# Modulation products behind their sums, and new places for VectorE and ScalarE work, in a three-layer float32 network

## The chip, the cores and the metric

The kernel runs on one core of a Trainium2 chip. The metric is the device time of one execution in microseconds (us); smaller is better. Inputs and outputs are float32 in the chip's main memory. TensorE multiplies in the fp32r type: each float32 matrix is held as a sum of two such values, "hi" and "lo", and a product is made of three matmuls (hi x hi, lo x hi, hi x lo).

## The reference, cut to what matters

512 tokens `x` and 256 context tokens, width 1024, pass two layers whose norms are modulated by a vector `c`, then a third block without modulation.

```python
for layer in range(2):
    mod_x = split(silu(c) @ ada_w[layer] + ada_b[layer], 6)       # ada_w: 1024 x 6144 a layer
    mod_c = split(silu(c_ctx) @ ada_w[layer] + ada_b[layer], 6)   # layer 1 needs mod_c[0], mod_c[1] only
    hx = rms_norm(x, norm1_g[layer]) * (1 + mod_x[1]) + mod_x[0]
    # layer 0: mLSTM heads with gate scans, beside a short gated convolution, over context and x
    # layer 1: 16 query heads in groups on 4 key heads, rms_norm and rope on q and k, softmax
    x = x + mod_x[2] * mixer(hx)
    x = x + mod_x[5] * mlp(rms_norm(x, norm2_g[layer]) * (1 + mod_x[4]) + mod_x[3])   # relu squared, hidden 4096
# third block
u = rms_norm(x, norm_mix_g) @ w_in
mixed = concat(rms_norm(stick_breaking(u)), rms_norm(conformer_conv(u)), rms_norm(s5_ssm(u)))
x = x + mixed @ w_out
x = x + cross_attention(x, mem);  x = x + gated_ffn(x)
```

Stick-breaking attention has 8 heads and takes, for each score, a softplus and then sums of the softpluses of all later keys.

## The kernel before, in words

TensorE (PE) does nearly everything that takes time, in an order written out by the program and, outside the grouped attention and the sums of stick-breaking, refined by a scheduler. The other engines feed it. Each engine takes its instructions in the order given.

**Weights.** `load_w` brings a unit of up to 2048 columns a partition by one DMA of SP's queue into `wst`; ScalarE (ACT) casts it to `whi` (L347), VectorE (DVE) subtracts to `wlo` (L348), in four pieces of 528, 528, 528 and 464 columns. `fm` (matmuls L310) and `tm` (L340) are the two loops of products. `split(hi, lo, src, ce, se)` is this pair of instructions for any tensor: `ce`, ACT by default, casts (L347), `se`, VectorE by default, subtracts (L348).

**Modulation.** `ada_v` makes `silu(c) @ ada_w` off TensorE: for each of six items of 1024 columns it brings rows of `ada_w` through two staging tiles (`ada`) and multiplies and adds them into accumulators `mac` (DVE, L500; the first row by ACT). In layer 0 an item has two variants (for x and for the context), two halves, four row pairs each. When both halves of an item are summed, sixteen or eight small matmuls (`ada_rows`, L472) gather the accumulators of all partitions, and `ada_end` writes `mods` (L458, L465). There are four `mac` buffers. `ada_v` is a generator, one step for each row pair, in the list `fillers`; `pump()` takes one step, and `fm` and `tm` pump behind each unit of weights (`steps`), or amid a product where `mix` is given.

**MLP of layer 0.** 8 blocks of 512 hidden columns: in each, four products with `w1` (m0 to m3 here), whose results go through ACT (relu and square) and a split into `h` on DVE (L347 cast, L348 subtraction), then eight products with `w2` that read `h`. Their results are added to x by DVE (L570). Layer 1's modulation runs in `fillers` beside them, two steps behind each unit.

**Around grouped attention.** `AT_ORD` is a string read from the left before the attention loop: a digit u is the query projection `q_proj(u)`, t a step of `key_turn` (transposes L1098 of keys, casts L1103), r a step of the rope of `q_rope(0)` (L1060, L1072, L1073), p a step of `at_prep(0)`. A capital letter hands the generator to `waiting`, and `fm`/`tm` then step it amid products (`wait_step`). `at_prep(c)` transposes queries (L1123), casts them (L1129, L1130), takes row maxima of scores (matmuls L1139, reductions L1140), turns these (L1149) and casts them (L1151) as a row of `QL` that the scores L1159 need. It yields after each of eight score tiles but the first, and `N_Y` = 3 times before L1149.

**Third block.** `sb_prep` makes queries and keys of stick-breaking heads (transposes L1643 and L1647, ACT L1650 and L1656, DVE L1651 and L1657); `sb_scores` makes scores (L1669 to L1671) and softplus (ACT L1677 and L212, DVE L1680, split); L1773 sums and ACT makes weights `w` (L212); L1787 multiplies values. `yhl` is the state-space branch's output, split, which the product `ssm_glu_w` reads; `OC` holds the convolution branch's output (`ev_pw`, L1725). `stage` brings the first 256 columns of a weight matrix early, in `ada` tiles, and its `part(i)` splits a quarter.

## Time and profile before

| | |
|---|---|
| median of 3 runs | 2483.6 us (2482.04 to 2489.34) |
| profiled execution | 2484.28 us, of which the span (first to last instruction) 2482.5 us and 1.78 us outside it |
| mean granted TensorE clock | 0.989 of full speed |
| busy: PE, DVE, ACT, POOL | 98%, 63%, 38%, 5% of the span |

A time at an instruction is from the start of the span. "Idle before" is how long its engine stood before it, and what released it. [...]

### The profile page before, as it was taken

Reading aid. Unit: us, or ns where it says so; the run is one execution under the profiler, and the core shown is the slowest. Engines: PE = TensorE matmul, PEld = TensorE weight load, DVE = VectorE, ACT = ScalarE, POOL = GpSimd, SP = SyncE. Lnnn points to the kernel's source line nnn. Section 1 sums busy time; section 2 is a strip of 40 time slices with the busy share of each in tenths; the row PEclk is TensorE's granted clock in tenths of the full one; section 3 lists DMA queues with packets and bytes.
Section 4 is the critical chain, followed back from the end, with each engine's and each line's share of the span. In section 5 each row is a group of like instructions: output and inputs, shape, how many; then the busy total and the mean of one; then the engine's idle time right before and its main releaser. Section 6 shows DMA issues by size and latency. Waiting matters only on the chain.

```text
span 2482.5 us, 34516 instructions
## 1 busy us (share of the span) xinstructions
PE 2424.4 (98%) x13648; PEld 2005.8 (81%) x13648; DVE 1572.1 (63%) x3300; ACT 940.8 (38%) x1982; POOL 118.9 (5%) x172
## 2 busy tenths in 40 slices
PE   7999999999999999999999999999999999999999
PEld 6978889888888889954487888886877977888887
DVE  5688467565543336799777775488767666543442
ACT  4322563322222214456543232342486534322321
POOL 0000110000000000133200000000000000000000
PEclk9999999999999999999999999999999999999999
DMA  7535034245442122100222323333103522323322
GB/s 249 171 111 161 1 102 136 69 127 171 145 136 68 52 68 86 56 1 1 66 93 87 116 85 102 102 102 99 57 1 128 178 69 85 102 74 105 101 86 93
DMA packets 214770, 238.46 MB, mean 96 GB/s; under 512 B 10704, under 2 KB 166992, under 8 KB 214608
## 3 DMA queue, kind: packets, MB, share of 16 engines
q1 hardware_dynamic: 212880, 233.19, 29.5%
q10 hardware_dynamic: 1728, 3.07, 0.3%
q8 instruction: 107, 1.75, 0.3%
q14 instruction: 55, 0.45, 0.1%
HBM read 225.63 MB, written 8.39 MB: 94 GB/s over the span
## 4 chain that ended last, share of the span: by engine, by line
PE 87%; DVE 7%; ACT 2%; DMA 2%; POOL 1%; issue 1%; SPq 0%; ACTq 0%; POOLq 0%; DVEq 0%
PE ps L310 65%; PE ps L340 6%; PE ps L897 2%; PE ps L646 2%; DMA ada<-ada_w 1%; PE ps L1249 1%; PE ps L865 1%; DVE mx L1140 1%; PE ps L1773 1%; PE ps L1557 1%; PE ps L1159 1%; DVE wlo L348 1%; PE ps L395 1%; PE ps L386 1%; PE ps L1468 1%
## 5 line engine op out<-in xcount | busy, mean ns | idle before, releaser
L310 PE MATMUL ps<-a,whi 128*128 128x512 f32 (+1 forms) x3784 | 986.7, 356 | 2.5 <-ACT a L405 1.4
L310 PEld LDWEIGHTS ps<-a,whi 128*128 128x128 f32 x3784 | 641.8, 189 | 111.4 <-issue 7.6
L310 PE MATMUL ps<-a,wlo 128*128 128x512 f32 (+1 forms) x1980 | 641.1, 357 | 0.0
L347 ACT CAST whi<-wst 128x528 fp32r<-128x528 f32 (+3 forms) x611 | 338.2, 610 | 579.0 <-PE ps L310 481.6
L310 PE MATMUL ps<-h,whi 128*128 128x512 f32 (+1 forms) x1776 | 458.0, 353 | 3.8 <-DVE h L347 3.7
L348 DVE TENSOR_TENSOR wlo<-wst,whi 128x528 fp32r<-128x528 f32 (+3 forms) x611 | 391.3, 677 | 77.5 <-ACT whi L347 76.5
L310 PEld LDWEIGHTS ps<-a,wlo 128*128 128x128 f32 x1980 | 346.5, 189 | 54.8 <-issue 1.9
L310 PEld LDWEIGHTS ps<-h,whi 128*128 128x128 f32 x1776 | 295.8, 189 | 54.7 <-DVE h L347 7.5
L310 PE MATMUL ps<-h,wlo 128*128 128x512 f32 (+1 forms) x800 | 239.1, 349 | 0.0
L570 DVE SCALAR_TENSOR_TENSOR a<-ps,mods,a 128x512 f32<-128x512 f32 (+1 forms) x200 | 122.2, 641 | 156.0 <-PE ps L310 155.4
L340 PE MATMUL ps<-whi,a 128*128 128x256 f32 (+1 forms) x1024 | 191.2, 285 | 0.6 <-ACT a L1590 0.6
L500 DVE SCALAR_TENSOR_TENSOR mac<-ada,sc,mac 128x512 f32<-128x512 f32 x224 | 158.5, 748 | 37.7 <-DMA ada<-ada_w 21.4
L340 PEld LDWEIGHTS ps<-whi,a 128*128 128x128 f32 x1024 | 160.8, 191 | 11.3 <-issue 7.9
L310 PEld LDWEIGHTS ps<-h,wlo 128*128 128x128 f32 x800 | 134.6, 189 | 19.7
L340 PE MATMUL ps<-wlo,a 128*128 128x256 f32 (+1 forms) x512 | 145.3, 285 | 0.5 <-DVE wlo L348 0.5
L559 ACT ACTIVATE t<-ps 128x512 f32<-128x512 f32 x60 | 35.9, 598 | 256.4 <-PE ps L310 243.9
L347 DVE CAST h<-t 128x512 fp32r<-128x512 f32 x60 | 25.5, 425 | 149.7 <-ACT t L561 149.7
L340 PEld LDWEIGHTS ps<-wlo,a 128*128 128x128 f32 x512 | 97.6, 191 | 2.1 <-issue 1.1
L352 POOL TENSOR_TENSOR sm<-sm,mhalf 128x2 f32<-128x2 f32 (+2 forms) x27 | 28.5, 1056 | 973.4 <-DVE sm L388 970.3
L212 ACT ACTIVATE p<-ps 128x512 f32<-128x512 f32 x96 | 53.8, 596 | 40.1 <-PE ps L1160 30.2
L1140 DVE TENSOR_REDUCE mx<-ps 128x1 f32<-128x512 f32 (+1 forms) x128 | 62.8, 550 | 4.9 <-PE ps L1139 4.6
L2021 DVE TENSOR_TENSOR a<-a,ps 128x512 f32<-128x512 f32 x16 | 11.0, 688 | 79.9 <-PE ps L310 79.9
(433 smaller groups left out, 2974.2 us busy)
## 6 DMA issues: line engine op xcount, KB each, us to landing
wst<-mlp_w SPq DMA_DIRECT2D x64, 1024.0 KB, 5.1
ada<-ada_w SPq DMA_DIRECT2D x80, 512.0 KB, 4.1
wst<-ffn_w_in SPq DMA_DIRECT2D x20, 1024.0 KB, 5.0
wst<-ffn_w_out SPq DMA_DIRECT2D x16, 704.0 KB, 4.2
wst<-hyb_w_in SPq DMA_DIRECT2D x10, 1024.0 KB, 5.6
wst<-w_in SPq DMA_DIRECT2D x9, 1024.0 KB, 5.2
a<-ada_w SPq DMA_DIRECT2D x32, 256.0 KB, 5.4
wst<-att_w_in SPq DMA_DIRECT2D x6, 1024.0 KB, 5.0
```

The source lines that it names most:

```text
L212: i = A.activation(out, in_, func, **kw)
L310: T.matmul(p, w(k, slice(m, m + P)), tiles[t][i // 2][:, s:s + n], start=(k == k0 and i == 0), stop=(k == k1 and i == 2))
L340: T.matmul(p, tiles[i // 2][:, s:s + P], (wl if i == 1 else wh)(k, slice(0, n)), start=(k == 0 and i == 0), stop=(k == KC - 1 and i == 2))
L347: last["copy"] = (ce.copy if ce is A else ce.tensor_copy)(hi, src)
L348: return se.tensor_tensor(lo, src, f(hi), ALU.subtract)
L352: G.tensor_tensor(r, v, mhalf[:, :n], ALU.pow)
L500: V.scalar_tensor_tensor(m, x, s, m, op0=ALU.mult, op1=ALU.add)
L559: A.activation(r, p, AF.Relu)
L570: V.scalar_tensor_tensor(xs, p, mod(l, 5)(c, v), xs, op0=ALU.mult, op1=ALU.add)
L646: T.matmul(vp[n_][:, u * 256:(u + 1) * 256], act[k][t][i // 2][:, s:s + P], (lo if i == 1 else hi)[:, k, :], start=(k == 0 and i == 0 and ...
L897: T.matmul(o, x, VS[:, kt, h, :], start=(n_ == 0), stop=(n_ == len(terms) - 1))
L1140: V.tensor_reduce(MX[:, e, t, i:i + 1], z, AX.X, ALU.max)
```

## The change

Four edits. (1) In `ada_v` the gathering matmuls of an item may come `ADA_LATE` = 2 steps behind its last sum, if the accumulators held meanwhile fit in the buffers; layer 0 gets six `mac` buffers, so all its items come two steps later; in layer 1 with four buffers items 2 to 5 do. (2) The MLP of layer 0 pumps amid each `w1` product (behind its fourth of eight row blocks) instead of behind each `w1` unit, and not at all in block 0's `w1` products. (3) `AT_ORD` is written anew: two key turns fewer and the maxima sooner; the rest of the key turns is handed to the products; in the first turn of `at_prep` only every second score tile yields, and `N_Y` there is 1. (4) In the third block the key casts of `sb_prep`, the copy out of `ev_pw` and the casts of the staged `w_out` go from ACT to DVE, and the splits of `yhl` stand before the projection of values.

```diff
+ADA_LATE = 2
-AT_ORD = "1ttttrrrr2pppP3"
+AT_ORD = "1ttrrrrT2pP3"
-    def stage(src):
+    def stage(src, ce=A):
-            split(*hl, sts[i // 2][:, (i % 2) * 512:(i % 2 + 1) * 512])
+            split(*hl, sts[i // 2][:, (i % 2) * 512:(i % 2 + 1) * 512], ce)
-                                if mix and k % mix == mix - 1:
+                                if mix and (k == at if at is not None else k % mix == mix - 1):
                                     pump()
-    def ada_v(fp, l, its, after=None):
+    def ada_v(fp, l, its, after=None, bufs=4):
+        late = []
+        def end(i, vs, accs):
+            p = ps()[:, :256]
+            for v in vs:
+                ada_rows(p, pick[:, v, :], lambda j: accs[j // 2][v][:, (j % 2) * 256:(j % 2 + 1) * 256], v == 0, v == vs[-1])
+            ada_end(l, i, p)
...
             if k0 == KC - 2 and h:
-                p = ps()[:, :256]
-                for v in vs:
-                    ada_rows(p, pick[:, v, :], lambda j: accs[j // 2][v][:, (j % 2) * 256:(j % 2 + 1) * 256], v == 0, v == vs[-1])
-                ada_end(l, i, p)
+                held = len(vs) * 2 + (len(range(2 if l == 0 or i + 1 < 2 else 1)) * (2 if l else 1))
+                late.append((n_ + (ADA_LATE if held <= bufs else 0), (i, vs, accs)))
+            if late and late[0][0] <= n_:
+                end(*late.pop()[1])
+            yield
+        if late:
+            end(*late.pop()[1])
             yield
-            fm(w1[:, b * blk * P:(b + 1) * blk * P], KC, act, rngs, evac1, c0=b * blk, first=groups if b == 0 else None, steps=steps)
+            fm(w1[:, b * blk * P:(b + 1) * blk * P], KC, act, rngs, evac1, c0=b * blk, first=groups if b == 0 else None,
+               steps=0 if amid else steps, mix=amid and b > 0, at=3 if amid else None)
-    fillers.append(ada_v(fp, 0, range(2, 6), began))
+    fillers.append(ada_v(fp, 0, range(2, 6), began, 6))
-                if (e, t) != (0, 0):
+                if (t % 2 if c == 0 else (e, t) != (0, 0)):
                     yield
-        for _ in range(N_Y):
+        for _ in range(N_Y if c else 1):
             yield
-                A.copy(ks[u], k[u])
+                V.tensor_copy(ks[u], k[u])
+    yhl = new_act(2, False)
+    for c in range(2):
+        split(*yhl[c][0], Y[c])
     psum.close()
     psum = open_psum(6)
...
-        A.copy(OC[c], items[0][1])
+        V.tensor_copy(OC[c], items[0][1])
-    staged = stage(a["w_out"][:, 0:256])
+    staged = stage(a["w_out"][:, 0:256], V)
```

In layer 0, DVE's queue behind the gate scans reads so before the change (L753 to L767 belong to the scans; `mac_1727` is the last sum of the item whose gathering matmuls come next on PE, `wlo_2008` a weight unit that PE reads soon):

```order
L753 SCALAR_TENSOR_TENSOR a_1780<-a_1774,a_1781 4x512
L756 SCALAR_TENSOR_TENSOR a_1780<-a_1774,a_1781 4x512
...
L766 TENSOR_SCALAR a_1819<-a_1781 64x256
L500 SCALAR_TENSOR_TENSOR mac_1727<-ada_1872,sc,mac_1727 128x512
L767 SCALAR_TENSOR_TENSOR a_1819<-a_1781,a_1819 64x256
L500 SCALAR_TENSOR_TENSOR mac_1952<-ada_1902,sc,mac_1952 128x512
L500 SCALAR_TENSOR_TENSOR mac_1953<-ada_1902,sc,mac_1953 128x512
L465 TENSOR_TENSOR mods_92<-ps_1919,cols 128x8 x2
L348 TENSOR_TENSOR wlo_2008<-wst_2006,whi_2007 128x528 x3
```

And so in the changed kernel, whose lines stand 2 to 15 further down here (L511 is L500, L350 is L348, L768 to L782 are the scans):

```order
L768 SCALAR_TENSOR_TENSOR a_1780<-a_1774,a_1781 4x512
L771 SCALAR_TENSOR_TENSOR a_1780<-a_1774,a_1781 4x512
...
L781 TENSOR_SCALAR a_1819<-a_1781 64x256
L511 SCALAR_TENSOR_TENSOR mac_1937<-ada_1938,sc,mac_1937 128x512
L782 SCALAR_TENSOR_TENSOR a_1819<-a_1781,a_1819 64x256
L511 SCALAR_TENSOR_TENSOR mac_1936<-ada_1938,sc,mac_1936 128x512
L511 SCALAR_TENSOR_TENSOR mac_1937<-ada_1938,sc,mac_1937 128x512
L350 TENSOR_TENSOR wlo_2008<-wst_2006,whi_2007 128x528 x3
```

The last sum of the item has gone from behind the scans to ahead of them; what stands behind them now are sums of the next item and then the weight unit.

In the MLP of layer 0, block 2, DVE's queue around the split of m3's result (`h_6170`, `h_6172`) reads so before:

```order
L500 SCALAR_TENSOR_TENSOR mac_6612<-ada_6613,sc,mac_6612 128x512 x2
L500 SCALAR_TENSOR_TENSOR mac_6612<-ada_6617,sc,mac_6612 128x512 x2
L500 SCALAR_TENSOR_TENSOR mac_6612<-ada_6763,sc,mac_6612 128x512
L347 CAST h_6170<-t_6175 128x512
L500 SCALAR_TENSOR_TENSOR mac_6612<-ada_6763,sc,mac_6612 128x512
L348 TENSOR_TENSOR h_6171<-t_6175,h_6170 128x512
L347 CAST h_6172<-u_6181 128x256
```

And so now (`h_6161`, `h_6163` are the same tensors):

```order
L511 SCALAR_TENSOR_TENSOR mac_6300<-ada_6301,sc,mac_6300 128x512
L511 SCALAR_TENSOR_TENSOR mac_6300<-ada_6305,sc,mac_6300 128x512 x2
L349 CAST h_6161<-t_6166 128x512
L511 SCALAR_TENSOR_TENSOR mac_6300<-ada_6433,sc,mac_6300 128x512
L350 TENSOR_TENSOR h_6162<-t_6166,h_6161 128x512
L349 CAST h_6163<-u_6172 128x256
```

One staged tile's sums stood between two tiles' sums and the cast; now the cast stands ahead of the first sum of the next staged tile, and the rest of the split behind it.

Late in stick-breaking, ACT's queue between a head's softplus (`t`) and the weights `w` of the head before it reads so before:

```order
L1677 ACTIVATE t_17898<-ps_17864 128x384
L347 CAST a_17905<-ada_17383 128x512
L212 ACTIVATE t_17898<-t_17898 128x384
L347 CAST a_17911<-t_17913 128x512
L212 ACTIVATE t_17898<-t_17898 128x384
L212 ACTIVATE w_17929<-ps_17771 128x512
```

And so now (L1692 is L1677, L214 is L212, L1804 is L1789):

```order
L1692 ACTIVATE t_17898<-ps_17864 128x384
L214 ACTIVATE w_17929<-ps_17771 128x512
L214 ACTIVATE t_17898<-t_17898 128x384
L214 ACTIVATE w_17937<-ps_17770 128x384
L214 ACTIVATE t_17898<-t_17898 128x384
L214 ACTIVATE w_17947<-ps_17769 128x512
```

The staged cast is gone to DVE, the cast `a_17911` stands behind the next head's softplus, and `w` comes straight behind L1692.

## Rows read from the trace of the kernel before

**Rows 1.** the page: busy us, share of the span, instructions by engine

```profile
PE 2424.4 (98%) x13648; PEld 2005.8 (81%) x13648; DVE 1572.1 (63%) x3300; ACT 940.8 (38%) x1982; POOL 118.9 (5%) x172
```

**Rows 2.** windows: length, busy us by engine, granted clock, DMA share, GB/s

```profile
262.00:269.00 7.00, 7.00 (x26) 5.56 (x26) 3.25 (x5) 4.42 (x12) 0.00 (x0) 0.51 0.00 0
176.60:183.60 7.00, 5.26 (x18) 3.89 (x19) 5.66 (x13) 0.37 (x1) 0.00 (x0) 0.51 0.46 135
610.20:613.80 3.60, 2.97 (x10) 2.58 (x11) 3.43 (x8) 0.72 (x1) 0.00 (x0) 0.53 0.52 152
1051.00:1080.00 29.00, 24.23 (x179) 22.23 (x180) 28.08 (x70) 11.90 (x31) 8.83 (x25) 1.00 0.00 1
1079.00:1228.00 149.00, 143.17 (x584) 68.59 (x586) 137.32 (x247) 96.94 (x173) 54.30 (x56) 1.00 0.00 1
1815.00:1818.60 3.60, 3.13 (x15) 3.13 (x16) 2.98 (x6) 3.60 (x9) 0.00 (x0) 0.53 0.00 0
1866.20:1873.20 7.00, 7.00 (x25) 5.88 (x24) 4.35 (x9) 5.99 (x13) 0.00 (x0) 0.51 0.01 2
```

**Rows 3.** timeline, PE in layer 0: start, length, instruction, idle before and releaser

```profile
178.34 1.07 PE L472 MATMUL ps<-mac,pick 128*32 128x256 f32 x4 [4.14 <-DVE mac L500]
...
260.13 0.39 PE L870 MATMUL ps<-a,a 128*128 128x256 f32 x1 [1.05 <-DVE a L832]
```

**Rows 4.** timeline, DVE in the same layer

```profile
127.61 2.50 DVE L348 TENSOR_TENSOR wlo<-wst,whi 128x528 fp32r<-128x528 f32 x4 [11.47 <-ACT whi L347]
...
177.55 0.73 DVE L500 SCALAR_TENSOR_TENSOR mac<-ada,sc,mac 128x512 f32<-128x512 f32 x1
```

**Rows 5.** timeline, PE in block 2 of layer 0's MLP

```profile
609.37 0.49 PE L310 MATMUL ps<-h,whi 128*128 128x512 f32 x1 [1.86 <-DVE h L347]
610.83 0.58 PE L310 MATMUL ps<-h,whi 128*128 128x256 f32 x1 [0.97 <-DVE h L347]
```

**Rows 6.** timeline, DVE in the same block

```profile
608.22 0.75 DVE L500 SCALAR_TENSOR_TENSOR mac<-ada,sc,mac 128x512 f32<-128x512 f32 x1 [2.41 <-DMA ada<-ada_w]
```

**Rows 7.** timeline, PE ahead of grouped attention

```profile
1060.26 0.97 PE L1139 MATMUL ps<-a,a 128*128 128x512 f32 x4 [1.34 <-ACT a L1129]
...
1064.50 0.39 PE L1139 MATMUL ps<-a,a 128*128 128x256 f32 x1 [0.69 <-DVE mx L1140]
...
1078.97 0.47 PE L1159 MATMUL ps<-a,a 65*128 65x512 f32 x1 [1.80 <-ACT a L1151]
```

**Rows 8.** groups of DVE lines, 1036 to 1228 us: busy, mean ns | idle

```profile
L1072 DVE TENSOR_TENSOR a<-a,a 128x256 f32<-128x256 f32 x19 | 10.8, 583 | 1.5 <-POOL u L1071 1.5
L1073 DVE TENSOR_TENSOR a<-a,u 128x256 f32<-128x256 f32 x20 | 10.3, 530 | 0.1
...
L1060 DVE TENSOR_TENSOR a<-a,sm 128x256 f32<-128x256 f32 x16 | 7.0, 480 | 0.1
```

**Rows 9.** timeline, PE in stick-breaking

```profile
1780.39 0.39 PE L340 MATMUL ps<-wlo,a 128*128 128x256 f32 x1 [0.29 <-DVE wlo L348]
...
1787.00 0.50 PE L310 MATMUL ps<-a,whi 128*128 128x512 f32 x1 [1.07 <-ACT a L347]
...
1815.47 1.11 PE L1643 MATMUL ps<-kst,a 128*128 128x128 f32 x4 [1.68 <-ACT a L1725]
...
1864.03 0.38 PE L1669 MATMUL ps<-a,a 128*128 128x256 f32 x1 [2.15 <-ACT w L212]
```

**Rows 10.** timeline, ACT in stick-breaking

```profile
1814.84 1.06 ACT L1725 COPY a<-ps 128x512 f32<-128x512 f32 x2
...
1861.46 0.67 ACT L347 CAST a<-ada 128x512 fp32r<-128x512 f32 x1
...
1863.33 1.51 ACT L212 ACTIVATE w<-ps 128x512 f32<-128x512 f32 x3
```

**Rows 11.** timeline, DVE in stick-breaking, and by shape its casts out of PSUM

```profile
1814.97 0.69 DVE L1680 SCALAR_TENSOR_TENSOR t<-ps,t 128x512 f32<-128x512 f32 x1 [1.21 <-ACT t L212]
...
L1103 DVE CAST a<-ps 64x512 fp32r<-64x512 f32 x4 | 2.7, 684 | 0.1
```

More of the change, by code (lines that the diff above doesn't have):

```diff
@@ L276, in load_w, with fm @@
         return [lambda k, c, x=x.rearrange("p (k n) -> p k n", k=kc): x[:, k, c] for x in (hi, lo)]
-    def fm(src, kc, act, rngs, evac, c0=0, koff=0, ksplit=None, first=None, last=None, done=None, then=None, steps=1, mix=0, tag="mm"):
+    def fm(src, kc, act, rngs, evac, c0=0, koff=0, ksplit=None, first=None, last=None, done=None, then=None, steps=1, mix=0, tag="mm", at=None):
         ncols = src.shape[1]
@@ L488, in ada_v @@
             if k0 == 0:
-                accs = (accs if h else []) + [[fp.tile([P, 512], F32, tag="mac", name=nm("mac"), bufs=4) for _ in vs]]
+                accs = (accs if h else []) + [[fp.tile([P, 512], F32, tag="mac", name=nm("mac"), bufs=bufs) for _ in vs]]
             if n_ + 1 < len(todo):
@@ L546, in norm_late, with mlp @@
         return put, done, ready, rc, rb
-    def mlp(l, act, X, rngs, groups, blk, acc, done, steps, then, new=s2, put=None):
+    def mlp(l, act, X, rngs, groups, blk, acc, done, steps, then, new=s2, put=None, amid=False):
         w1, w2 = a["mlp_w1"][l], a["mlp_w2"][l]
@@ L993, in body @@
     mlp(0, lambda k: act[k], X, FXC, GXC, 4, acc2, norm_spill, 2, a["att_w_in"][0][:, 1024:1280],
-        lambda dt: fp.tile([P, 512], dt, tag="h", name=nm("h"), bufs=N_H))
+        lambda dt: fp.tile([P, 512], dt, tag="h", name=nm("h"), bufs=N_H), amid=True)
     finish()
@@ L1696, in body @@
     v_proj(0)
-    yhl = new_act(2, False)
-    for c in range(2):
-        split(*yhl[c][0], Y[c])
     ya = {}
```

## Prediction, made before the changed kernel was run

> **What bounds the kernel now.** First the page's busy shares: PE is busy for 2424.4 of the span's 2482.5 us [rows 1], so all engines together cost it some 58 us of standing still, and the change, which leaves PE's matmuls as they are, can win no more than a part of these 58 us and what the clock loses. Second, the windows of half clock: the granted clock is 0.51 to 0.53 in a few stretches of 3.6 or 7 us, 1.00 elsewhere around the places of this change [rows 2]; in a stretch at 0.51 PE gets through half its matmuls, so 7 us of steady matmuls lose 3.4 us and 3.6 us lose 1.7. Third, the timeline of PE, for the waits: the reader is to look at the bracket, which gives PE's idle time and who ended it [rows 3, 5, 7, 9]. Fourth, DVE and ACT ahead of each such wait: what they did instead. Waits and half clock belong together: PE stood 4.14 us at 178.34, and the clock is half from 176.6; 2.83 us at 609.37 and 610.83, and it is half from 610.2; 1.68 us at 1815.47, half from 1815.0; 2.15 us at 1864.03, half from 1866.2 [rows 2, 3, 5, 9].
>
> **Edit 1, products of layer 0 two steps later.** PE waited 4.14 us at 178.34 for the last sum into `mac` [rows 3]; DVE did that sum at 177.55, behind the gate scans [rows 4]. In the change's order this sum stands ahead of the scans. Six buffers also let the sums run ahead: DVE stood idle for 11.47 us before 127.61 [rows 4], which is where the extra sums go, so they cost nothing. -4.14. The half clock to 183.6 costs 0.49 of the 5.26 us in which PE worked in it [rows 2]: -2.6. What is late next: behind the scans DVE now has two whole sums (0.73 us each [rows 4]) ahead of the weight unit `wlo`, which PE reaches sooner, as it no longer stops. The sum at 177.55 stood among the last of the scans [rows 4], which so ended near 178.7; with the sums that go ahead of them I estimate 0.5 us more, 179.2; two sums end at 180.6, the first piece of `wlo` is there at 181.2, and PE, counted by the matmuls that its order has ahead and 4.14 us early, wants it near 180.0. A new wait of 1.2 us, between 0 and 2.5. Sum -4.1 - 2.6 + 1.2 = -5.5; from -6.7 to, with the clock falling all the same, -1.6. The wait of 1.05 us at 260.13 is for another tensor [rows 3] and stays.
>
> **Edit 2, steps amid the `w1` products of layer 0's MLP.** The waits at 609.37 and 610.83 are for the cast and the split of `h` on DVE, queued behind sums that themselves stood 2.41 us for a transfer of `ada_w` [rows 5, 6]. In the change's order the cast stands ahead of the first sum of the late tile, the rest of the split behind it. -1.86 - 0.97 = -2.8, and the clock: half for 3.6 us with 2.97 us of work in it [rows 2], -1.4. Not all of the pattern is gone: in blocks 1 and 2 the next tile's sum still stands between the cast and the split's subtraction, or ahead of the narrow part. A step's load goes into SP's queue when it is pumped, now in the middle of a product, so its tile is late by less than before; each of these two waits lies between nothing and the 2.41 us by which a tile was late [rows 6]. I take 0.9 us in block 1, where only the narrow part is behind a late sum, and 1.2 us in block 2, the middle. Later blocks have their sums amid the `w2` products, where a late L570 frees PSUM later but no `h` waits; nothing is taken, and the slower rival has the price. Sum -2.8 - 1.4 + 2.1 = -2.1; from -4.2 to +1.7.
>
> **Edit 3, the order ahead of grouped attention.** Waits of 1.34, 0.69 and 1.80 us [rows 7] were for casts and maxima of the first `at_prep`, which no other matmul covered; now twelve matmuls stand between the turned maxima L1149 and the first scores L1159, and the maxima run amid `q_proj(3)`. -3.8. The price is on DVE: from 1051 to 1080 it is busy 28.08 of 29 us, and in the attention 137.32 of 149 [rows 2]. Maxima that come sooner push rope into the attention: in the two orders four L1060, three L1072 and three L1073 move behind the start of the scores, 4 x 0.48 + 3 x 0.58 + 3 x 0.53 = 5.3 us [rows 8]. DVE's 11.7 idle us there can hold it if they lie well; PE did not wait for DVE there before. Bounds: nothing, or 5.3 us. I take 2.0, nearer to nothing since the idle time is twice the work. Sum -1.8; from -3.8 to +1.5.
>
> **Edit 4, casts to DVE and `yhl` sooner.** At 1787.00 PE waited 1.07 us for ACT's cast of `yhl` [rows 9]; it now comes ahead of everything there. But the two subtractions that go with it stand ahead of `wlo` on DVE, which PE already waited 0.29 us for at 1780.39: one more of 0.65 us there. -0.4. At 1815.47 PE waited 1.68 us for ACT's copy of `OC` at 1814.84, while DVE stood idle for 1.21 us up to 1814.97 [rows 9 to 11]: on DVE that copy runs in the idle time and ends about 1.1 us sooner. -1.1, and the half clock there (3.13 us of work at 0.53 [rows 2]) -1.5. At 1864.03 PE waited 2.15 us for ACT's `w` at 1863.33; in the new order two casts (0.67 us each) and two softplus steps no longer stand ahead of it, so it can start near 1861.5 to 1861.9, and about 0.25 us of the wait is left [rows 9, 10]. -1.9, and the 7 us at 0.51 [rows 2], -3.4. DVE takes over eight key casts, two copies and four staged casts: at 0.68 us for the dearest like them [rows 11] at most 9.6 us over a stage in which it has more idle time than that; in the softplus chain these are hidden behind PE's sums, and if that cover were gone the cost would be a part of those. Sum -0.4 - 2.6 - 5.3 = -8.3; from -10 to -0.5 (the clock falls all the same, and half of the waits come back).
>
> **The clock as a risk.** Four small waits remain: 1.2, 0.9, 1.2 and 0.6 us. Three waits of that size stand in the rows, 1.05, 1.34 and 1.07 us [rows 3, 7, 9]: after the first the clock is half from 262 to 269, around the second it is 1.00 throughout [rows 2], and after the third no such stretch follows. So one of the four is taken to bring 7 us of half clock, +3.4.
>
> [...]
>
> **The sum.** -5.5 - 2.1 - 1.8 - 8.3 + 3.4 = -14.3 us on the profiled execution's 2484.3 us, which lies 0.7 us above the median of 2483.6 us. From the median: 2469.3 us; I say 2469.5.
>
> **Rivals.** *New waits eat the middle.* The sums in blocks 1 and 2 cost 2.1 us each with the clock as before (4.2 - 2.8), DVE in attention passes on the 5.3 us, stick-breaking's later waits shift rather than go. For it: DVE's 28.08 of 29 us ahead of attention [rows 2], and that each wait removed was the last of several that end close together. Against: DVE is at 63% overall [rows 1]. Edit 1 -4.1, edit 2 +1.4, edit 3 +1.5, edit 4 -3: -4.2, some 2479.4 us. [...] *Slower: late transfers meet the split of `h` in every block.* The pumps now all lie in `w1` products of blocks 1 to 7, and a step whose transfer is late holds DVE's queue, with `h` or the weights' `wlo` behind it. Each block then pays what block 2 paid before, 2.83 us and 1.4 of clock [rows 2, 5]: x blocks cost 4.2 (x - 1) more than now. With -5.5 - 1.8 - 8.3 from the other edits, the gain is gone from x = 5, and it is slower by over 0.3% only at x = 7, some 2493 us. Against: in the order most sums of later blocks stand amid the `w2` products. *It doesn't do what it says:* the last sum of layer 0 is ahead of the scans in the order, so the wait can't stay as it was.
>
> **Chances.** What a measurement of this kernel can tell is about 0.3%, 7.5 us: faster means under 2476.1. Forecast, 2462 to 2476 us: 0.60. Clock not back: 0.11. New waits: 0.23. Slower or near it by the transfers: 0.06, of which 0.04 beyond 0.3%. Of the forecast and the clock case nearly all lies below 2476: faster 0.71, within 0.3% 0.25, slower 0.04. The range reaches from the sum with all clock back and no new wait in edits 1 and 2 (2483.6 - 17.7 - 3.3 = 2462.6, less a little for edit 3) to the new waits and a little beyond: 2461 to 2481.
>
> **What would show it.** Edit 1: L472 without a wait near 175, a clock of 1.00 there, and a wait of about 1 us on `wlo` some 2 us on. Edit 2: no wait of 1.86 us in the MLP's third block, waits on L310 near 1 us in the second and third. Edit 3: no wait at L1159, L1139 waits under 0.7, and PE waits on DVE inside the attention adding up to 2 us. Edit 4: waits at L1643 under 0.8 us and at L1669 near 0.3, no half clock from 1800 to 1870. Wrong would be: a half clock that moves only by a few us, PE waits on `h` in several blocks, or a new wait on L348 over 2 us in stick-breaking.

## The result, and the profile after

The changed kernel took 2501.18 us, median of 4 runs (2497.13 to 2504.8), beside 2484.55 us of the kernel before (4 runs, 2482.04 to 2489.34): ratio 1.0062, 95% interval 1.0047 to 1.0077. It is slower by 15.4 us, twice the 7.3 us over which the four runs of the kernel before spread, and outside the range 2461 to 2481.

The page of the changed kernel, busy us by engine, against [rows 1]: PE's busy time grew by 8.3 us although it does the same 13648 matmuls.

```profile
span 2499.0 us, 34511 instructions
...
PE 2432.7 (97%) x13648; PEld 2008.5 (80%) x13648; DVE 1579.4 (63%) x3314; ACT 933.4 (37%) x1968; POOL 119.9 (5%) x172
```

Matmuls take longer where the clock is halved: two 128x512 L312 take 0.51 us at 213.57 (granted clock 1.00 from 213 to 214) and 0.84 at 223.12 (0.50 from 223 to 224). Added up over windows of 1 us, each 1 minus its granted clock, the span before lost 26.5 us to half clock, the span after 35.8, so 9.3 more. PE's waits from 100 us on, added up from its timeline, are 35.8 us before and 44.2 after, 8.4 more. Together 17.7, for a span that grew by 16.5: a stretch at half clock that falls into a wait counts twice. By stage, PE's waits and what the half clock took:

| stage (positions before) | waits before | after | half clock before | after |
|---|---|---|---|---|
| layer 0, 100 to 366 | 8.1 | 9.3 | 15.4 (from 0) | 18.8 (from 0) |
| MLP of layer 0, to 1052 | 4.6 | 3.0 | 1.7 | 0 |
| ahead of attention, to 1079 | 5.7 | 4.0 | 0 | 0 |
| attention, to 1285 | 5.0 | 10.6 | 0 | 8.5 |
| MLP of layer 1, to 1754 | 4.0 | 3.9 | 3.4 | 1.7 |
| third block, to 1950 | 8.2 | 13.0 | 5.1 | 6.8 |

The windows of the changed kernel that answer to [rows 2] (columns as there):

```profile
177.00:185.00 8.00, 7.82 (x57) 6.11 (x56) 7.95 (x14) 3.51 (x9) 0.00 (x0) 1.00 0.42 116
219.00:227.00 8.00, 5.65 (x20) 4.88 (x21) 7.20 (x16) 3.54 (x7) 0.00 (x0) 0.57 0.52 153
263.00:281.00 18.00, 17.81 (x69) 15.17 (x69) 7.82 (x16) 8.99 (x29) 0.91 (x2) 0.53 0.00 0
612.00:616.00 4.00, 2.91 (x17) 2.40 (x17) 4.00 (x9) 1.16 (x2) 0.00 (x0) 1.00 0.36 128
1051.00:1076.40 25.40, 22.52 (x175) 21.28 (x175) 23.15 (x55) 11.00 (x30) 0.73 (x2) 1.00 0.00 1
1083.00:1090.00 7.00, 6.99 (x16) 3.49 (x16) 5.81 (x13) 1.50 (x3) 0.00 (x0) 0.51 0.00 0
1107.00:1114.00 7.00, 6.56 (x16) 3.63 (x16) 4.89 (x11) 1.80 (x4) 1.27 (x1) 0.52 0.00 0
1130.00:1135.00 5.00, 5.00 (x15) 2.52 (x16) 5.00 (x11) 1.20 (x2) 3.00 (x2) 0.66 0.00 0
1830.00:1841.00 11.00, 10.01 (x29) 7.42 (x30) 6.46 (x12) 5.50 (x12) 0.00 (x0) 0.53 0.01 1
```

The half clock near 178 and 610 is gone, as forecast. New are 219 to 227, three stretches in the attention, which stood at 1.00 throughout in [rows 2], and 1830 to 1841; the stretches of before at 1815 and 1866 are not there. The stretch behind 262 has grown from 7 to 18 us.

**Layer 0** (PE, then ACT, DVE and the waits of SP's queue from 205 to 224). L474, L460, L457, L507 and L511 are L472, L458, L455, L496 and L500 of before.

```profile
178.55 1.07 PE L474 MATMUL ps<-mac,pick 128*32 128x256 f32 x16
180.35 0.62 PE L312 MATMUL ps<-a,wlo 128*128 128x512 f32 x2 [0.18 <-DVE wlo L350]
...
214.36 1.07 PE L474 MATMUL ps<-mac,pick 128*32 128x256 f32 x16
221.35 0.69 PE L460 MATMUL ps<-kst,u 128*128 128x128 f32 x2 [5.02 <-ACT u L457]
260.03 0.39 PE L885 MATMUL ps<-a,a 128*128 128x256 f32 x1 [1.04 <-DVE a L847]
```

```profile
220.31 0.72 ACT L507 ACTIVATE mac<-ada,sc 128x512 f32<-128x512 f32 x1 [5.17 <-DMA ada<-ada_w]
220.94 0.35 ACT L457 COPY u<-ps 128x256 f32<-128x256 f32 x1
```

```profile
213.67 5.38 DVE L511 SCALAR_TENSOR_TENSOR mac<-ada,sc,mac 128x512 f32<-128x512 f32 x8
```

```profile
SPq L493 <- DVE mac L511: 13.4, 4, 6.2
```

The wait of 4.14 us [rows 3] is gone from 178, and one of 5.02 us stands at 221. To be read backwards: PE's transposes L460 need the copy L457 of the gathered sums. ACT stood still for 5.17 us, since ahead of L457 in its queue stood L507, the first row of a new tile of `ada_w`. That tile's load waited 6.2 us in SP's queue, the longest of the four waits in that row, until DVE had read the staging tile, and DVE's eight sums, which now come in a bunch, run from 213.67 to 219.05. In the kernel before, this copy (L455) also came behind such a first row (L496), but that row waited only for PE's L472 to free its accumulator; its tile was there in time, and the transpose (L458) had no wait:

```profile
214.09 0.72 ACT L496 ACTIVATE mac<-ada,sc 128x512 f32<-128x512 f32 x1 [5.76 <-PE ps L472]
214.72 0.35 ACT L455 COPY u<-ps 128x256 f32<-128x256 f32 x1
```

```profile
215.12 0.44 PE L458 MATMUL ps<-kst,u 128*128 128x128 f32 x2
```

**MLP of layer 0**, where [rows 5] stood:

```profile
613.19 0.39 PE L312 MATMUL ps<-h,whi 128*128 128x256 f32 x1 [1.09 <-DVE h L349]
```

**Grouped attention**, PE from 1060 (L1154 is L1139, L1174 is L1159):

```profile
1063.69 0.39 PE L342 MATMUL ps<-whi,a 128*128 128x256 f32 x1 [1.66 <-DVE mx L1155]
1076.38 0.47 PE L1174 MATMUL ps<-a,a 65*128 65x512 f32 x1 [0.59 <-ACT a L1043]
...
1082.72 0.92 PE L1154 MATMUL ps<-a,q 128*128 128x512 f32 x2 [1.89 <-DVE mx L1155]
1105.45 0.72 PE L1154 MATMUL ps<-a,q 128*128 128x512 f32 x2 [2.02 <-DVE mx L1155]
1128.06 0.38 PE L1154 MATMUL ps<-a,q 128*128 128x256 f32 x1 [0.89 <-DVE mx L1155]
1150.81 0.71 PE L1154 MATMUL ps<-a,q 128*128 128x512 f32 x2 [1.42 <-DVE mx L1155]
```

The scores start 2.6 us sooner, at 1076.38 instead of 1078.97 [rows 7]. Then PE waits in four turns for the maxima of the next turn. In the kernel before, PE waited for such maxima too, ten times and 3.7 us in all, but the longest of these waits was 0.61 us:

```profile
1084.08 0.72 PE L1139 MATMUL ps<-a,q 128*128 128x512 f32 x2 [0.61 <-DVE mx L1140]
```

DVE in the changed kernel ahead of the second of these waits (L1087 is L1072), and POOL beside it:

```profile
1096.19 1.25 DVE L364 TENSOR_SCALAR sm<-sm 128x16 f32<-128x16 f32 x1
1097.36 0.16 DVE L1070 TENSOR_SCALAR v<-QS 128x16 f32<-128x16 f32 x1
1097.48 1.23 DVE L365 TENSOR_TENSOR sm<-sm,sm 128x16 f32<-128x16 f32 x1
1098.74 1.22 DVE L1075 TENSOR_TENSOR a<-a,sm 128x256 f32<-128x256 f32 x3
1100.73 0.53 DVE L1087 TENSOR_TENSOR a<-a,a 128x256 f32<-128x256 f32 x1 [0.77 <-POOL u L1086]
1102.03 0.53 DVE L1087 TENSOR_TENSOR a<-a,a 128x256 f32<-128x256 f32 x1 [0.77 <-POOL u L1086]
...
1104.73 1.60 DVE L1155 TENSOR_REDUCE mx<-ps 128x1 f32<-128x512 f32 x3
```

```profile
1095.75 2.92 POOL L1274 TENSOR_TENSOR p<-p,p 128x512 f32<-128x512 f32 x2 [14.10 <-DVE p L1272]
1099.31 4.35 POOL L1086 TENSOR_TENSOR u<-a,a 128x64 f32<-128x64 f32 x12 [0.64 <-DVE a L1075]
```

This is the norm and rope chain of a later query projection. It stands between the first turn's probabilities and the next turn's maxima: DVE is at it from 1096.19 to 1103.5, 1.54 us of that in two round trips to POOL and 2.48 us in two operations on 128x16 values. One operation on probabilities and a cast of queries follow, and then the maxima at 1104.73. In the kernel before, only rope pieces of 3.9 us stood at this place (1095.02 to 1098.94), and the maxima came at 1100.28.

**Third block**, PE (L1658, L1684 are L1643, L1669):

```profile
1790.16 0.38 PE L342 MATMUL ps<-wlo,a 128*128 128x256 f32 x1 [0.89 <-DVE wlo L350]
1822.67 0.66 PE L1658 MATMUL ps<-kst,a 128*128 128x128 f32 x4 [0.64 <-DVE a L1740]
1828.34 0.63 PE L1658 MATMUL ps<-kst,a 128*128 128x128 f32 x4 [1.58 <-DVE a L1666]
1830.99 0.55 PE L1684 MATMUL ps<-a,a 128*128 128x256 f32 x1 [2.02 <-DVE a L1672]
1903.17 0.95 PE L312 MATMUL ps<-a,a 128*128 128x512 f32 x3 [1.03 <-ACT a L349]
1928.50 0.50 PE L312 MATMUL ps<-a,wlo 128*128 128x512 f32 x1 [2.77 <-DVE wlo L350]
```

Of the four waits of [rows 9], 1.07 and 2.15 us are gone, 1.68 has become 0.64, 0.29 has become 0.89. Three longer waits are new: 1.58 and 2.02 us for queries and keys of stick-breaking, and 2.77 us for a weight unit behind it; the 1.03 us at 1903.17 was 0.34 before.

### The profile page after: what moved, and what is told of

Its sections match the earlier page's. It is cut to its first block, busy times and chain, and to the rows that moved or that the text cites. A ratio compares the mean times of both kernels' runs of the same rounds, so it can differ in the third digit from the quotient of the medians.

```text
span 2499.0 us, 34511 instructions
## 1 busy us (share of the span) xinstructions
PE 2432.7 (97%) x13648; PEld 2008.5 (80%) x13648; DVE 1579.4 (63%) x3314; ACT 933.4 (37%) x1968; POOL 119.9 (5%) x172
## 4 chain that ended last, share of the span: by engine, by line
PE 86%; DVE 8%; DMA 2%; ACT 2%; SPq 1%; POOL 1%; issue 1%; ACTq 0%; POOLq 0%; DVEq 0%
PE ps L312 63%; PE ps L342 7%; PE ps L912 2%; PE ps L661 1%; PE ps L1264 1%; PE ps L880 1%; DVE mac L511 1%; DMA ada<-ada_w 1%; DVE wlo L350 1%; PE ps L1174 1%; PE ps L1788 1%; PE ps L1154 1%; PE ps L1572 1%; PE ps L397 1%; DVE mx L1155 1%
## 5 line engine op out<-in xcount | busy, mean ns | idle before, releaser
L312 PE MATMUL ps<-a,whi 128*128 128x512 f32 (+1 forms) x3784 | 986.7, 356 | 2.0 <-ACT a L407 1.4
L312 PEld LDWEIGHTS ps<-a,whi 128*128 128x128 f32 x3784 | 641.5, 189 | 108.2 <-issue 4.7
L312 PE MATMUL ps<-a,wlo 128*128 128x512 f32 (+1 forms) x1980 | 638.6, 356 | 3.2 <-DVE wlo L350 3.2
L312 PE MATMUL ps<-h,whi 128*128 128x512 f32 (+1 forms) x1776 | 457.8, 353 | 2.2 <-DVE h L349 2.1
L350 DVE TENSOR_TENSOR wlo<-wst,whi 128x528 fp32r<-128x528 f32 (+3 forms) x611 | 390.4, 675 | 72.8 <-ACT whi L349 71.8
L312 PEld LDWEIGHTS ps<-a,wlo 128*128 128x128 f32 x1980 | 346.1, 189 | 59.2 <-DVE wlo L350 4.0
L312 PEld LDWEIGHTS ps<-h,whi 128*128 128x128 f32 x1776 | 294.9, 188 | 53.7 <-DVE h L349 6.0
L312 PE MATMUL ps<-h,wlo 128*128 128x512 f32 (+1 forms) x800 | 238.6, 347 | 0.0
L511 DVE SCALAR_TENSOR_TENSOR mac<-ada,sc,mac 128x512 f32<-128x512 f32 x224 | 158.1, 746 | 30.6 <-DMA ada<-ada_w 15.1
L312 PEld LDWEIGHTS ps<-h,wlo 128*128 128x128 f32 x800 | 134.3, 188 | 19.7
L573 ACT ACTIVATE t<-ps 128x512 f32<-128x512 f32 x60 | 35.9, 598 | 274.5 <-PE ps L312 262.0
L214 ACT ACTIVATE p<-ps 128x512 f32<-128x512 f32 x96 | 53.7, 596 | 46.2 <-PE ps L1175 37.6
```

What stands on the lines that cost most here:

```text
L214: i = A.activation(out, in_, func, **kw)
L312: T.matmul(p, w(k, slice(m, m + P)), tiles[t][i // 2][:, s:s + n], start=(k == k0 and i == 0), stop=(k == k1 and i == 2))
L350: return se.tensor_tensor(lo, src, f(hi), ALU.subtract)
L511: V.scalar_tensor_tensor(m, x, s, m, op0=ALU.mult, op1=ALU.add)
L573: A.activation(r, p, AF.Relu)
```

## The experiments

Each variant is the kernel before with the edit named, unless said otherwise. Times are medians; "before" ran on the same chip beside them. A ratio's interval is 95%. A ratio differs a little from the quotient of the two medians, and a change in us is worked out from the ratio (e2: 0.17% of 2485.58 is 4.2 us).

**One edit at a time.** Four variants, one for each edit (layer 1's late products went with edit 2):

```diff
-                late.append((n_ + (ADA_LATE if held <= bufs else 0), (i, vs, accs)))
+                late.append((n_ + (ADA_LATE if l == 0 and held <= bufs else 0), (i, vs, accs)))   # e1: layer 0 alone
```

> Only the modulation of layer 0 late, with six mac buffers; everything else as before. Theory A (the stages' differences between the two traces add up): the wait of 4.14 us at L472 goes, a wait of about 5 us comes at the transposes of ada_end (L458) because ACT's copy of their input stands behind a product on a late tile; +1 to +5 us, about +3. Theory B (the loss of the whole change comes from half clock that falls by chance, not from this order): within 1.5 us of the kernel before. Prediction as it was made: -5.5 us.

> Only the MLP of layer 0: steps amid the w1 products, and items 2 to 5 of layer 1's modulation two steps late. Theory A: the stage from 371 to 1051 us is 5.3 us shorter in the changed trace, so -5.3 us, -4 to -6.5. Theory B (that stage's gain is given back when the stages behind it start elsewhere): within 2 us. Prediction as it was made: -2.1 us.

> Only the order ahead of grouped attention and the fewer yields of the first turn. Theory A: two more rope turns on DVE and GpSimd in the attention hold up the maxima, PE waits at L1139 for them and its clock halves: 2.3 us won ahead of the attention, 13 us lost in it, +10.7 us. Theory B (the waits matter, the half clock there is chance): 13 less 8.5 us of clock, so about +2 us. Prediction as it was made: -1.8 us.

> Only the third block: key casts, copy of OC and staged casts on DVE, yhl's splits ahead. Theory A: the waits at 1787.00 and 1864.03 go, waits of 1.6 and 2.0 us on DVE come near 1828 to 1831 and one of 2.8 us on a weight's wlo near 1928: +7 us (5 to 9). Theory B (the wait on wlo comes from the times at which the other edits let the scheduler stand, not from this one): +2 to +4 us and no wait over 1 us on wlo. Prediction as it was made: -8.3 us.

| variant | us | before | ratio | interval |
|---|---|---|---|---|
| e1, edit 1 in layer 0 | 2488.29 | 2485.58 | 1.0007 | 0.9998 to 1.0016 |
| e2, edit 2 and edit 1 in layer 1 | 2482.09 | 2485.58 | 0.9983 | 0.9973 to 0.9993 |
| e3, edit 3 | 2492.90 | 2485.58 | 1.0034 | 1.0021 to 1.0046 |
| e4, edit 4 | 2492.72 | 2485.58 | 1.0026 | 1.0015 to 1.0038 |

The ratios add up to +0.50%, 12.4 us, within the interval of the whole (11.7 to 19.1): the edits show no interaction beyond the noise, and each can be judged by itself. Theory A came true for e1, e2 and e4; e3 lies between its two theories, at +8.4 us. Each variant shows the waits of the changed kernel at its place: 5.11 us at L460 in e1; 1.90 and 2.03 us for maxima in e3, with half clock taking 8.5 us from 1081 to 1133; 1.58, 2.02 and 2.78 us in e4.

**Edit 1, one step late instead of two.** e1 with

```diff
-ADA_LATE = 2
+ADA_LATE = 1
```

> Layer 0's modulation with six buffers, but products one step behind the sums instead of two. In this order the last sum stands ahead of the scans as well, and ACT's copy for the transposes stands ahead of the product on the late tile. Theory A (the new wait of 5 us is that copy's place in ACT's queue): both waits are gone, -5 us (-4 to -7). Theory B (DVE and the transfers are late there whatever ACT's order is): a wait of 3 us or more stays at L458 or L472, and the time is within 2 us of the kernel before.

2480.43 us beside 2487.15: ratio 0.9971, 0.9959 to 0.9984. PE and ACT at the place where the changed kernel waits 5.02 us:

```profile
212.08 1.07 PE L474 MATMUL ps<-mac,pick 128*32 128x256 f32 x16
213.77 0.38 PE L460 MATMUL ps<-kst,u 128*128 128x128 f32 x2
```

```profile
213.22 0.37 ACT L457 COPY u<-ps 128x256 f32<-128x256 f32 x1 [6.11 <-PE ps L474]
...
220.00 1.34 ACT L507 ACTIVATE mac<-ada,sc 128x512 f32<-128x512 f32 x2 [6.01 <-DMA ada<-ada_w]
```

The tile is as late as in the changed kernel (220.00), but the copy now stands ahead of it: PE has no wait between 205 and 224 us, and from 170 to 255 us its clock is 1.00 throughout. So what undid edit 1 is the place of ACT's copy behind a late tile, not the six buffers or the sums: one step is a gain of 7.2 us (interval 4.0 to 10.2), two are none.

**Edit 3, where the loss sits.** Two variants with all of edit 3: e7 moves the ropes to later matmuls of the attention (by which queries of later projections are in part turned after they are read), e9 leaves out norm and rope of the second query projection.

```diff
-RG, ROPES, SG_AT, N_Y = ("q",), (-1, -1, 0, 0, 3, 4, 5, 6, 9, 10, 11, 12), 21, 3
+RG, ROPES, SG_AT, N_Y = ("q",), (0, 0, 1, 1, 6, 7, 8, 9, 13, 14, 15, 16), 21, 3        # e7
-    ropes = [q_rope(u) for u in (1, 2, 3)]
+    ropes = [iter(range(4)), q_rope(2), q_rope(3)]        # e9
```

> The edits ahead of attention, and the ropes of the other three query projections each some turns later in the attention (0, 0, 1, 1, 6 to 9, 13 to 16 in place of -1, -1, 0, 0, 3 to 6, 9 to 12). Theory A1 (the place of the second rope, whose DVE steps stand for GpSimd's products with the maxima queued behind them, makes the waits): the waits of 1.9 and 2.0 us go and at least 4 of the 8.4 us come back. Theory A2 (DVE has simply too much to do in the attention): the waits move, and the time stays within 2 us of that with the ropes where they were, +8.4 us.

> The edits ahead of attention, and the norm and rope of the second query projection left out (four turns, 6.4 us of DVE and their GpSimd products; those queries stay unturned). Theory A (DVE enters the attention with some 5 us of work more than before, and PE's maxima wait until it is worked off, with half clock beside the waits): the waits of 1.9, 2.0, 0.9 and 1.4 us at L1139 shrink to a sum under 2 us, no half clock there, and the time is 1 to 5 us under that of the kernel before. Theory B (the waits come from where the fewer yields put the matmuls of the maxima): they stay, +5 us or more.

e7: 2494.44 beside 2487.15, ratio 1.0032 (1.0019 to 1.0046), waits of 1.90 and 1.83 us. e9: 2490.11 beside 2486.75, ratio 1.0014 (1.0004 to 1.0024); the first wait stays at 1.93 us, the second is down to 0.48.

e7 hardly tests the place: on DVE a rope chain still stands directly ahead of the second maxima, 1096.97 to 1102.3 (in e3 1094.92 to 1102.2), and the waits add up to 10.6 us as in e3. In e9, PE's waits from the first scores to 1265 fall to 6.9 us: 0.48 has one of 1.06 us right behind it, and the later waits of 0.89 and 1.40 are gone. The first stays, and a rope chain of another projection (1082.51 to 1088.9) stands on DVE ahead of those maxima. So a part of the waits is DVE's load; neither theory of e9 holds in full, as 3.5 us of loss remain.

Then the parts of edit 3: the fewer yields alone (e10), the string alone (e13), and the fewer yields with the maxima handed to the products while all key turns stay ahead (e14):

```diff
-AT_ORD = "1ttttrrrr2pppP3"
+AT_ORD = "1ttrrrrT2pP3"        # e13, yields as before
+AT_ORD = "1ttttrrrr2pP3"       # e14, with the fewer yields
```

> Of the edits ahead of attention only the fewer yields of the first turn, with the order string as before. Theory A (DVE's work is pushed into the attention by the sooner start that both parts make): something between, waits ahead of attention down by 1 to 2 us and waits in it up by 2 to 4, 0 to +4 us. Theory B (the yields alone make the loss): +8 us.

> Edit 3's order string alone, the first turn of at_prep yielding as often as before. Theory (the loss sits in the string: it puts rope and key casts of VectorE behind the start of the scores): 0.3 to 0.45% above before, waits of about 1.9 and 2.0 us on the next turn's maxima some 6 and 29 us behind the first scores, half clock beside them. Rival (it takes string and fewer yields together): within 0.1% of before and none of the two waits.

> Edit 3 with its fewer yields and the maxima amid the products (P for the last p's), but all key turns ahead of the rope as before: 1ttttrrrr2pP3. Theory (the key casts that are moved amid the products push the rope chain of the next turns behind the first scores): the two waits near 2 us inside the attention are gone or under 1 us, time within 0.1% of before or up to 0.1% below it. Rival (it is the maxima being moved amid q_proj(3), not the keys): both waits stay and it is 0.2 to 0.35% above before.

| variant | us | before | ratio | interval | waits from 1035 to the first scores, then to 1260 |
|---|---|---|---|---|---|
| before's profile | | | | | 5.7, 5.0 |
| e3, all of edit 3 | 2492.90 | 2485.58 | 1.0034 | 1.0021 to 1.0046 | 4.1, 10.6 |
| e10, yields | 2484.45 | 2486.75 | 0.9990 | 0.9981 to 0.9999 | 4.5, 4.9 |
| e13, string | 2489.38 | 2486.73 | 1.0009 | 0.9997 to 1.0021 | 6.5, 6.7 |
| e14, yields and maxima | 2492.68 | 2486.73 | 1.0028 | 1.0018 to 1.0039 | 3.1, 11.1 |

Neither theory of e10 came true: the waits ahead go down by 1.2 us, and none come behind. e13 failed its theory, and its rival held: alone, the string costs 0.09% or nothing, and no wait of 1.9 us stands in the attention; it stands ahead of it (1.90 us at L1149, 1.33 at L1159). e14 failed its theory too, and its rival held: with the key turns where they were, both waits are there.

```profile
1076.29 0.48 PE L1159 MATMUL ps<-a,a 65*128 65x512 f32 x1 [0.59 <-ACT a L1028]
...
1082.63 0.72 PE L1139 MATMUL ps<-a,q 128*128 128x512 f32 x2 [1.89 <-DVE mx L1140]
...
1105.53 0.71 PE L1139 MATMUL ps<-a,q 128*128 128x512 f32 x2 [2.01 <-DVE mx L1140]
```

And in e10, where three steps of the maxima stay ahead of `q_proj(3)`:

```profile
1083.38 0.47 PE L1159 MATMUL ps<-a,a 65*128 65x512 f32 x1 [0.55 <-ACT a L1028]
...
1088.46 0.72 PE L1139 MATMUL ps<-a,q 128*128 128x512 f32 x2 [0.63 <-DVE mx L1140]
```

So it takes both halves: the maxima handed to the products after one step, and the fewer yields (the former without the latter was run only together with the later key turns, e13). Then the scores start when DVE is only 2.9 us into the rope chains (at L1055, 1073.44 in e14) instead of 5.7 us (1077.69 in e10), and the rest of the chains, with their round trips to POOL, goes into the attention ahead of the next maxima. Against e10, e14 saves PE 1.4 us before the scores and costs it 6.1 us behind them.

**Edit 4, which casts.** The staged casts alone (e5), the key casts alone (e6), edit 4 without the key casts (e11), key and staged casts alone (e15):

```diff
-    staged = stage(a["w_out"][:, 0:256])
+    staged = stage(a["w_out"][:, 0:256], V)        # e5, e11, e15
-                A.copy(ks[u], k[u])
+                V.tensor_copy(ks[u], k[u])        # e6, e15
```

> Of the third block's edits only the casts of the staged w_out go to DVE. Theory A (each wait belongs to the edit in whose queue it stands): ACT's weights w start earlier, the wait of 2.15 us at 1864.03 goes, nothing comes at L1651, L1657 or on wlo: -2 us, with the clock behind it -5. Theory B (the four edits only work together, and the order of DVE behind stick-breaking is upset by this one): a wait of 2.8 us on wlo near 1920, so 0 to +2 us.

> Of the third block's edits only the key casts go to DVE. Theory A: these make the two waits of 1.6 and 2.0 us at L1643 and L1669 (for L1651 and L1657, behind three softplus steps on DVE), with half clock behind them: +3 to +6 us. Theory B (those waits come from the copy of OC that stands ahead of them on DVE): within 1.5 us.

> The third block's edits without the key casts. Each of the key casts and the staged casts by itself left the time as it was (-0.8 and -0.5 us), while all four made +6.5. Theory A (the key casts, together with the copy of OC ahead of them in DVE's queue, make the waits of 1.6 and 2.0 us and the shift of the order behind them that ends in the wait of 2.8 us on wlo): those three waits are gone, -2 to -6 us. Theory B (the splits of yhl and the copy of OC make the loss by themselves): +3 us or more.

> Key casts and staged casts on VectorE, the rest of edit 4 left out. Theory (the 2.8 us wait on wlo behind the last output product needs these two together, each alone had none): a wait of 2.5 to 3 us on wlo there, time 0.1 to 0.2% above before. Rival (it needs the OC copy or the early yhl split as well): no such wait, within 0.1% of before.

| variant | us | before | ratio | interval | waits: `w` L212 / keys L1657 / `wlo` |
|---|---|---|---|---|---|
| before's profile | | | | | 2.15 / none / none |
| e4, all of edit 4 | 2492.72 | 2485.58 | 1.0026 | 1.0015 to 1.0038 | none / 2.02 / 2.78 |
| e5, staged | 2485.81 | 2487.15 | 0.9998 | 0.9985 to 1.0010 | 1.22 / none / 0.23 |
| e6, key | 2486.22 | 2487.15 | 0.9997 | 0.9986 to 1.0009 | 0.87 / 2.07 / none |
| e11, without key | 2486.96 | 2486.75 | 0.9999 | 0.9989 to 1.0009 | 1.22 / 0.96 / 0.23 |
| e15, key and staged | 2488.91 | 2486.73 | 1.0015 | 1.0001 to 1.0028 | none / none / 2.77 |

e5 and e6 each came true in part: the time hardly moves, but in e5 the wait on `w` is not gone, and in e6 the wait for the keys comes all the same:

```profile
1819.52 0.36 PE L1669 MATMUL ps<-a,a 128*128 128x256 f32 x1 [2.07 <-DVE a L1657]
```

That e15 shows none for the keys does not clear the key casts. DVE's operations there are in e6's order, but in e15's profile PE ran at half clock from 1813.0 to 1819.8 and came to L1669 only at 1820.99, when the key subtraction had just ended. Neither theory of e11 came true: without the key casts the time is that of before, with waits of 1.59 and 0.96 us left. e15's theory held.

Staged casts take the wait on `w` from 2.15 to 1.22 us, key casts to 0.87, both together remove it. But both together also turn DVE's queue behind stick-breaking round: in e15, as in the changed kernel, PE waits 2.77 us at the last output product.

```profile
1915.75 0.80 PE L310 MATMUL ps<-a,wlo 128*128 128x512 f32 x1 [2.77 <-DVE wlo L348]
```

The order of the changed kernel has the fourth piece (464 columns) of that unit behind 16 operations of the mean and variance work there, before it stood ahead of them. Neither the staged nor the key casts alone are worth anything that can be measured; the key casts in company make the loss, since without them (e11) it is gone. e15 has 3.7 us of e4's 6.5; the copy of `OC` and the early `yhl` were not run with the key casts alone, so the rest is not divided further.

**Parts that help, together.** Edit 2, edit 1 with layer 1 two steps and layer 0 one step late (e12); the same with the fewer yields (e16); edit 4 and the string left out of both:

```diff
-                late.append((n_ + (ADA_LATE if held <= bufs else 0), (i, vs, accs)))
+                late.append((n_ + ((ADA_LATE if l else 1) if held <= bufs else 0), (i, vs, accs)))
```

> What the experiments left as gains: the steps amid the w1 products with layer 1's modulation two steps late, and layer 0's modulation with six buffers one step late; nothing of the attention's and the third block's edits. If the gains add: -4.2 - 7.2 = -11.4 us (-8 to -14), under both kernels. If the second takes from the first (the stage behind it stands elsewhere): -7 us.

> Edit 2, layer 0 one step late, and the fewer yields of edit 3, without its string and without edit 4. If the gains add as they did so far: 0.39% and 0.10%, so 0.45 to 0.5% below before, about 2475.5 us. If they don't: as without the fewer yields, 0.39% below.

e12: 2478.04 beside 2486.75, ratio 0.9961 (0.9949 to 0.9973). e16: 2474.37 (2468.48 to 2482.19, 6 runs) beside 2486.73, ratio 0.9952 (0.9935 to 0.9968). The gains add within the intervals, and both beat the two kernels; that e16 is better than e12 lies within the intervals.

**The half clock over all these kernels.** What it took in each profiled execution, us, worked out as above:

| | before | after | e3 | e7 | e9 | e14 | e13 | e10 | e12 | e16 |
|---|---|---|---|---|---|---|---|---|---|---|
| 0 to 400 | 15.4 | 18.8 | 11.9 | 11.9 | 18.8 | 15.4 | 18.8 | 18.8 | 8.5 | 13.6 |
| attention | 0 | 8.5 | 8.5 | 6.8 | 6.8 | 8.5 | 5.1 | 1.7 | 1.7 | 1.7 |
| whole span | 26.5 | 35.8 | 29.0 | 33.3 | 35.9 | 35.9 | 33.3 | 25.6 | 15.4 | 25.7 |

In the attention it is larger with the waits: 6.8 to 8.5 us in the five kernels with waits of about 2 us there, 0 to 5.1 in all the others. But it does not need them: in the ten profiles whose attention is that of before, with no wait over 0.81 us, it takes 0 to 5.1 us, 2.2 on average. Of e4's 5.1, 1.7 follow the wait of 1.80 us just ahead of the scores, and 3.4 stand beside waits of 0.53 us at most. So the 0 in the profile of before is at the low end of a spread. Two other places are clearer. A stretch near 178 stands in all 13 profiles without edit 1 in layer 0 and in none of the five with it; one in block 2 of layer 0's MLP, between 608 and 617, in 11 of 14 without edit 2 and in none of the four with it. From 0 to 400 us it took 11.9 to 20.5 us in the twelve variants without edit 1, whose program is nearly the same there, so a single profile's layer 0 proves little.

## Why the prediction was wrong, point by point

**Edit 1: -5.5 forecast, +1.7 measured (e1, interval -0.5 to +4.0).** The wait at 178 went as said, with its half clock, and the wait on `wlo` that was to take its place is 0.18 us, not 1.2. The failed step is "what is late next". It followed the late sums to DVE's next work only. The gathering has a second customer, ACT's copy behind it, and two steps later this copy stands on ACT's queue behind the first row of a tile whose load is still under way. [Rows 3, 4] do not show ACT; its queue around L455 was not read. e8 shows the cause: with the copy ahead of the late tile the wait is gone and the edit is worth 7.2 us; the interval, 4.0 to 10.2, holds the forecast's 5.5. The growth of the stretch behind 262 from 7 to 18 us in the changed kernel has no such cause: e5, which leaves layer 0 as it was, has a long one there as well (10.2 us lost from 261 to 283).

**Edit 2: -2.1 forecast, -4.2 measured (e2).** The mechanism was right, and the forecast lies within the interval (-6.7 to -1.7). Of the terms for new waits, block 2's +1.2 has its size, one wait of 1.09 us (1.36 in e2) in place of 2.83; block 1's +0.9 did not come (0.15), and nothing is left of the half clock. The slower rival (late transfers meeting `h` in every block) has no row for it: no other wait on `h` over 0.3 us in this MLP.

**Edit 3: -1.8 forecast, +8.4 measured (e3).** The gain was there: 1.7 of the 3.8 us ahead of the scores (1.80 became 0.59, and 1.34 and 0.69 went, but a wait of 1.66 for maxima came). The failed step is "I take 2.0, nearer to nothing since the idle time is twice the work". Its premise, "PE did not wait for DVE there before", was false: PE waited ten times there, 3.7 us in all, for DVE's maxima, so DVE's work ahead of those maxima was on PE's path already. Comparing work with idle time over 149 us says nothing about who stands ahead of whom: what moved was a chain through POOL, and it moved directly ahead of the maxima that PE needs next. The waits behind the start of the scores grew by 5.6 us, just above the upper bound of 5.3; what no bound had was the half clock, 8.5 us in this profile, 6.3 above the average of kernels with the attention of before. Less the 1.7 us gained, that is 10.2 us, within e3's interval of 5.2 to 11.4, and the half clock is no smaller a part than the waits.

**Edit 4: -8.3 forecast, +6.5 measured (e4).** Right: the waits at L1643 and L1669 that were to shrink did (0.64 us; gone), and the half clock at 1815 and 1866 went. The failed step is "in the softplus chain these are hidden behind PE's sums". The key casts hold up the key subtraction, which PE needs at 1831: 2.02 us (2.07 with them alone, e6). The 1.58 us at 1828 is there without them too (1.59 in e11, where ACT's `w` ends it) and not with the staged casts alone (e5); whether the copy of `OC` or the early `yhl` makes it was not told apart. The sum also had no term for the order behind stick-breaking: with key and staged casts on DVE the scheduler puts a weight piece last, 2.77 us (e15). The sign "no half clock from 1800 to 1870" fell with them: 1830 to 1841 is at 0.53. The text had named "a new wait on L348 over 2 us in stick-breaking" as what would make it wrong; it came on L1672 (L1657 of before) there, and on `wlo` just behind.

**The clock as a risk: +3.4 forecast.** One of four remaining waits was to bring 7 us of half clock. The allowance was for the waits that the sum had found. With the 8.9 us that edits 1, 2 and 4 were to bring back, the sum had the half clock at -5.5; between the two profiles it is +9.3, of which 3.4 stand in layer 0, where nearly the same code varies by more. The rival "new waits eat the middle" named the right places in attention and stick-breaking, but its price, -4.2 instead of -14.3, left new half clock out. For "clock not back" (0.11) no run shows a mechanism. What the runs showed: 1.00 from 612 to 616, where waits of 2.83 us had become one of 1.09; 0.51 from 1083 behind a wait of 1.89 us; and in e4 0.51 and 0.50 from 1124.0 and 1165.0, where no wait behind the first score is over 0.53 us.

What stays open: why the half clock in layer 0 varies between profiles of nearly the same code there, and whether in the attention the sum of the waits or the single wait near 2 us decides (e9, one of 1.93 us and 6.9 in all, lost 6.8 us to half clock; e13, none over 0.99 behind the first scores and 6.7 in all, lost 5.1).

## What to carry to other kernels

When work is moved later in an order, follow every instruction behind it on every engine, the copy out of PSUM too, and look for a DMA that stands ahead of it in that queue: here one step later was worth 7 us and two steps nothing that can be measured. When a wait is removed by letting PE start sooner, ask what the slower engine still has to do before PE's next request; with DVE at 28 of 29 us ahead, PE's earlier start saved 1.7 us there and cost 5.6 us of waits behind it, with half clock beside them. A handful of casts moved to a less busy engine is judged by the engine's order at the next product, not by its share of busy time. A wait that is gone from one profile is not proof: look whether half clock has made PE itself late there, as in e15.

## What the runs showed of the hardware

In the changed kernel, operations on 128x16 values take 0.17 us on DVE ahead of the attention (L363 to L365, 1041.25 to 1043.1), but 1.25 and 1.23 us where they start beside POOL's L1274 (rows above, 1096.19 and 1097.48). In the trace the two POOL instructions merged in the row at 1095.75 end at 1097.41 and 1098.67, the two slow DVE operations at 1097.44 and 1098.70: each ends 0.03 us behind the POOL instruction that it started in. The operation at 1097.36, which starts as the second POOL instruction does, takes 0.16 us. In the kernel before, one such operation fell there, L360 at 1115.56 with 1.24 us, and it too ends 0.03 us behind POOL's L1259 (1116.80 against 1116.77). The traces show this overlap and these ends; whether POOL makes the operations long, and why some are long and others not, no run here separates.

DVE's queue stood 0.77 us in each of two round trips of a rope piece through POOL, ahead of 1100.73 and 1102.03 in the changed kernel.

Half clock stood beside single waits of 1.89 and 2.02 us (after: 0.51 from 1083 to 1090, 0.52 from 1107 to 1114) as well as beside one of 5.02 (after: 0.57 from 219 to 227), and in e4's attention, 0.51 and 0.50 from 1124.0 and 1165.0, beside waits of 0.53 us at most.
